# A hybrid SSD and S5 layer: residuals and half of a weight split as accumulating transfers, Silu on ScalarE

## The chip, the cores and the metric

One Trainium2 chip, one of its cores. The metric is the device time of one execution, in microseconds (us); smaller is better. The kernel is one launch, and its inputs and outputs lie in the chip's main memory.

## The reference

One layer is applied to 1024 prompt frames and to 32 frames of a running stream (1056 columns in all), 1024 channels, all in float32:

```
P = RMSNorm_pre_mix(x) @ W_in                 # -> [z | xBC | dt | u]
SSD:  xBC = silu(causal_dwconv4(xBC));  h_t = exp(dt_t a) h_{t-1} + dt_t x_t B_t^T;  y_t = C_t h_t + D x_t
      ssd = grouped RMSNorm(y * silu(z))      # 8 heads x 64, 2 groups of B and C, state 128
S5:   h_t = lb * h_{t-1} + B u_t (complex, 32 groups x 64 states);  y = Re(C h) + D u;  s5 = GLU(gelu(y))
h = x + RMSNorm_post_mix([ssd | s5] @ W_out)
[g | v] = causal_dwconv3(RMSNorm_pre_ffn(h) @ W_up)        # 2 x 2816 channels
y = h + RMSNorm_post_ffn((gelu(g) * v) @ W_down)
```

The states and the last convolution columns are returned too.

## The kernel before, in words

**Layout and tiling.** Channels lie on the 128 partitions, frames along the free axis. The frames are cut into three chunks of 512, 272 and 272 columns; the first is block 0, the other two are block 1 (544 columns). A vector of 1024 channels is eight slabs of 128 partitions. Each float32 product is made of three passes of a rounded type: an operand is split into a high half (the rounded value) and a low half (the rest), and TensorE adds high x high, high x low and low x high. Weights come as tiles of 128x1024 from the tensor wt. For each tile SP, the queue of SyncE, loads the raw values (`w_load`), ScalarE copies them into the high half `wh`, which rounds, and VectorE subtracts to get the low half `wl` (`w_split`, line 713). Each of the three names has two buffers. The tiles in order are 16 of the input projection, then the output projection and the up projection; the down projection has functions of its own.

**Stages.** `prologue` loads x, makes the two halves `xh` and `xl` (line 1045), squares each slab on ScalarE and collects the squares (`flush`): where the slab's number is in the parameter `pairs`, GpSimd adds it to the square before it, else it becomes one more tensor of a list. `norm_cols` multiplies each tensor of that list by a column of ones (`onec`), 128 frames at a time, accumulating over the list in one bank. `norm_r` turns the sums into factors by some small VectorE steps (`rsq`, lines 603 to 626) and spreads these over the partitions with one more product (`spread`). The input projection follows, with the S5 preparation and scan beside it as side work (`s5_prep`, `s5_run`). z is gated in `evac_z` and the later columns of xBC are convolved in `conv_b`, both with a sigmoid made of Tanh. `ssd_front` makes the masks of the SSD decay, exponentials on ScalarE follow. `post(b)` computes h: each slab of the output projection `O[b]` is multiplied by the norm's factor (line 1659), GpSimd adds x (line 1660), and h is split and squared for the next norm. For block 0, h is also kept in a tensor h_dram in main memory. Then two FFN blocks run; `up_evac` writes the tile fext, whose two leading columns are copied from `halo`. `fin_mm` makes the down projection's last part with the squares, and `fin_out` and `apply` the outputs: ScalarE multiplies by the norm's weight, VectorE or GpSimd (by the parameter `fp`) multiplies by the factor, then adds h (lines 1891 and 1893), and SP stores the result in yT.

**Order.** `Plan` reads all instructions and their dependences, estimates a cost for each, schedules them by lists and fixes the order in every engine's own queue. ScalarE's order is chosen with a price for each change of function table. SP alone issues the transfers, in the planned order. An instruction that waits holds back all behind it on its engine.

Of the kernel before, what the change touches and what calls it, by code (L numbers as in the profile page):

```python
# [9 lines left out]
F32 = mybir.dt.float32  # L10
# [9 lines left out]
WA = 512  # L20
# [28 lines left out]
           cvat='run7', tcat=1, late_at=2, nsq=1, fg=(), fp=((1, 3), (1, 3), (3,)), fch=(0, (0, 1), 2), pfin=0, q0=0, q1=0, q2=0, nb=0,   # L49
           hv=(), av=(3,), post0=0.802, dn_at=((3, 0), (3, 1)), ob_at=22, sa=2, sb=1, y5b=0, cvb=2.11, msb=(1, 1, 2, 2, 2), pch0=(3,),   # L50
           pch1=(3,), pch2=(3, 4), pf=0, pb=500, pg=0, pn=500, pr=0, pairs=(1, 2, 3, 5, 6), cf=4, cb=1, cg=0, cf2=2, cb2=(0, 1), cg2=0, 
# [130 lines left out]
class Plan:  # L182
# [61 lines left out]
    def read(self):  # L244
# [97 lines left out]
    def cost(self, q, i, ia, oa):  # L342
        self.eng[q] = e = str(i.engine).split(".")[-1]
        kind = type(i).__name__
        n = max(self.free(a) for a, _ in ia + oa)
        if kind == "InstDMACopy":
            self.bytes[q] = 4 * int(np.prod([m for _, m in ia[0][0].ap]))
            self.dur[q], self.lat[q] = 0.06, 2.0
            return
        if kind == "InstMatmult":  # L350
            n, m = (self.free(a) for a, _ in ia[:2])
            if ia[0][0].dtype == F32R:
                d = max(0.43 * n + 6, 107 if m > 64 else 54)
            elif i.is_transpose:
                d = 112
            else:
                d = 2 * max(0.85 * n, 108) if m > 64 else 0.85 * n
            self.dur[q], self.lat[q] = d * 1e-3, 0.07
            return
        big = [a for a, _ in ia if self.free(a) > 1]  # L360
        ps = any(g[0].startswith(("ms", "pm")) for _, g in ia)
        if kind == "InstActivation":
            self.fset[q] = str(i.func).split(".")[-1]
            d = 0.19 + 0.00085 * n + 0.08 * (len(ia) > len(big))
        elif e == "Pool":
            self.shared[q] = len(big) > 1
            d = 0.21 + 0.00165 * n if len(big) > 1 else 0.12 + 0.0009 * n
        else:
            self.shared[q] = not ps and n > 8
            d = 0.15 + (0.00105 if ps or len(big) > 1 else 0.00053) * n  # L370
        self.dur[q] = d

    def schedule(self, rank, pre, suc, forward=True, gate=None):
# [12 lines left out]
        while todo:  # L386
# [28 lines left out]
            if self.bytes[q]:  # L415
                if forward:
# [3 lines left out]
                end[q] = max(s + self.lat[q], wire + 0.8)  # L420
                lanes = lanes[1:] + [end[q]]
# [37 lines left out]
def body(tc, xT, wt, wdt, vec, cst, dtp, hist4, hist3, h0ssd, s5p, s5bc, s5d, glu, glub,  # L459
# [245 lines left out]
    def w_split(n):  # L705
        while st["split"] <= min(n, len(seq) - 1):
# [6 lines left out]
            V.tensor_tensor(lo, r, hi.bitcast(F32), sub)  # L713
# [35 lines left out]
    h_dram = dram.tile([128, KD, WA], F32, name="hd")  # L749
# [40 lines left out]
    def conv_b():  # L790
        yield par["cvat"]
        n = EB - 3
        cwh = con.tile([128, 40], F32, name="cwh")
        V.tensor_scalar(cwh, vc("cw", 0, 40), 0.5, None, mult)
        for j in range(8):
            e = XB[1][:, j, :]
            o, th = tl(("bc", "PQ")[j % 2], [128, n], "xob"), e[:, 0:n]
# [9 lines left out]
    def evac_z(j, c, ps):  # L807
# [533 lines left out]
    def ssd_front(c):  # L1341
# [301 lines left out]
    def post(b):  # L1643
        HN[b] = xtiles(b)
        for c in BLKC[b]:
# [7 lines left out]
            for j in range(4):  # L1653
                xr = iot("xr")[:, :, :w]
                D.dma_start(xr, xT[:, 2 * j:2 * j + 2, t0:t0 + w])
                for kk in range(2):
                    k = 2 * j + kk
                    h = O[b][:, k, o:o + w]
                    V.scalar_tensor_tensor(h, h, vc("post_mix", k), r1, mult, mult)  # L1659
                    (V if k in par["hv"] else G).tensor_tensor(h, h, xr[:, kk], add)  # L1660
# [9 lines left out]
                if b == 0:  # L1670
                    D.dma_start(h_dram[:, 2 * j:2 * j + 2], O[b][:, 2 * j:2 * j + 2, o:o + w])
# [188 lines left out]
    def fin_out(c):  # L1860
# [13 lines left out]
        if c == 1:  # L1874
            ap = [(1, j) for j in par["fp"][1]] + [(1, j) for j in range(4) if j not in par["fp"][1]][:par["ia"]]
        elif c == 2:
            ap = [(1, j) for j in range(4) if j not in par["fp"][1]][par["ia"]:] + ap
        with ExitStack() as es:
            if c == 2:
                es.enter_context(tc.issue_after(last[0].ins))  # L1880
            for c_, j in ap:
                apply(c_, j)
                yield 0.9

    def apply(c, j):
# [13 lines left out]
    hrs = {}  # L1899

    def fin_block(b):
        if b == 0:
            for j, n in enumerate(("ext0", "ext1", "W0", "G0", "T0", "C0")):
                h = tl(n, [128, 2 if j < 2 else 1, 512], "hr")
                k = 2 * j if j < 2 else j + 2
                D.dma_start(h, h_dram[:, k:k + h.shape[1]])
                for i in range(h.shape[1]):
                    hrs[k + i] = h[:, i]
# [37 lines left out]
```

## Time and profile before

| | |
|---|---|
| median of the runs | 1296.92 us (1296.79 to 1300.04) |
| the profiled execution | 1294.34 us, its span 1292.4 us |
| mean granted clock of TensorE | 0.979 |
| TensorE busy (matmul) | 1225.8 us, 95% |
| VectorE busy | 1035.2 us, 80% |
| ScalarE busy | 574.5 us, 44% |
| GpSimd busy | 397.7 us, 31% |
| main memory read, written | 111.69 MB, 15.81 MB |

The busy times are those of one profiled execution; the span runs from its first to its last instruction, and the execution's own time has 1.9 us more around it. PE is TensorE, DVE VectorE, ACT ScalarE, POOL GpSimd, and SP the engine that issues the transfers. The granted clock is the share of full speed at which TensorE was allowed to run.

### The profile page before, as it was taken

What the parts mean: (1) busy time and instruction counts of PE and PEld (TensorE: products, weight loads), DVE (VectorE), ACT (ScalarE), POOL (GpSimd) and SP (SyncE); (2) the same over time, 40 slices, a digit from 0 to 9 for tenths busy, and PEclk for the clock granted to TensorE, in tenths of its full rate; (3) what the DMA queues carried; (4) which work ended last, traced back from release to release, by engine and by line L of the source; (5) the groups of instructions that cost most, each with busy time, mean ns of one, the idle gap of its engine ahead of it and who ended that gap; (6) DMA issues with size and microseconds to landing.
All of it is one profiled execution on the core that took longest, in us unless ns stands there. A gap on an engine that the chain in (4) does not pass through costs nothing.

```text
span 1292.4 us, 20981 instructions
## 1 busy us (share of the span) xinstructions
PE 1225.8 (95%) x7880; PEld 1105.6 (86%) x7880; DVE 1035.2 (80%) x1781; ACT 574.5 (44%) x979; POOL 397.7 (31%) x577
## 2 busy tenths in 40 slices
PE   6879999999998999999999999998999999999995
PEld 5768888888877888878977888887999999999994
DVE  7898887988988998987688977679577777777777
ACT  7236466554555555543444433353523333333243
POOL 5364554544146433211345110015111111111113
PEclk8989999999998999999999999999999999999997
DMA  7133323233434423234433333222323332222212
GB/s 220 57 96 99 96 76 114 79 106 93 124 105 164 152 91 99 81 104 137 153 99 123 122 99 98 95 85 82 117 81 98 99 98 82 95 86 83 82 52 70
DMA packets 66901, 132.14 MB, mean 102 GB/s; under 512 B 13936, under 2 KB 34800, under 8 KB 66800
## 3 DMA queue, kind: packets, MB, share of 16 engines
q1 hardware_dynamic: 66800, 130.81, 32.2%
q8 instruction: 62, 1.02, 0.3%
q14 instruction: 39, 0.32, 0.1%
HBM read 111.69 MB, written 15.81 MB: 99 GB/s over the span
## 4 chain that ended last, share of the span: by engine, by line
PE 79%; DVE 10%; POOL 3%; issue 3%; DMA 2%; ACT 1%; SPq 1%; DVEq 0%; ACTq 0%; POOLq 0%
PE pm L479 70%; PE ms L479 9%; DVE wl L713 1%; POOL pacc L1666 1%; POOL o L1660 1%; DVE o L1659 1%; SPq L1122 1%; DMA xst<-xT 1%; DVE scr L647 1%; DVE scr L646 1%; POOL oacc L1628 1%; PE ms L483 1%; DVE pq L996 1%; POOL hq L1164 0%; DVE yr L1104 0%
## 5 line engine op out<-in xcount | busy, mean ns | idle before, releaser
L479 PE MATMUL pm<-xh,wh 128*128 128x272 f32 (+1 forms) x1616 | 532.1, 330 | 15.9 <-ACT wh L535 8.7
L479 PE MATMUL pm<-xh,wl 128*128 128x272 f32 (+1 forms) x1616 | 531.1, 329 | 7.4 <-DVE wl L713 7.3
L479 PE MATMUL pm<-xl,wh 128*128 128x272 f32 (+1 forms) x1616 | 529.8, 328 | 1.7 <-DVE xl L1045 1.7
L479 PEld LDWEIGHTS pm<-xh,wh 128*128 128x128 f32 x1616 | 309.9, 192 | 37.8 <-ACT wh L535 8.7
L479 PEld LDWEIGHTS pm<-xh,wl 128*128 128x128 f32 x1616 | 309.0, 191 | 30.8 <-DVE wl L713 9.1
L479 PEld LDWEIGHTS pm<-xl,wh 128*128 128x128 f32 x1616 | 309.9, 192 | 24.4 <-DVE xl L1045 3.0
L535 ACT ACTIVATE wh<-raw 128x1024 fp32r<-128x1024 f32 x120 | 126.9, 1057 | 177.5 <-PE pm L479 109.5
L713 DVE TENSOR_TENSOR wl<-raw,wh 128x1024 fp32r<-128x1024 f32 x120 | 154.9, 1291 | 26.6 <-ACT wh L535 26.1
L479 PE MATMUL pm<-al,dh 128*128 128x272 f32 (+1 forms) x528 | 171.4, 325 | 0.6 <-DVE al L1751 0.6
L479 PE MATMUL pm<-ah,dh 128*128 128x272 f32 (+1 forms) x528 | 171.7, 325 | 0.3 <-ACT ah L535 0.3
L479 PE MATMUL pm<-ah,dl 128*128 128x272 f32 (+1 forms) x528 | 170.8, 324 | 0.0
L1793 DVE TENSOR_TENSOR acc<-acc,pm 128x272 f32<-128x272 f32 (+1 forms) x235 | 121.1, 520 | 53.6 <-PE pm L479 52.5
L1738 DVE SCALAR_TENSOR_TENSOR ftmp<-fext,vec_t,ftmp 128x512 f32<-128x512 f32 (+1 forms) x176 | 143.1, 814 | 3.9 <-ACT ftmp L535 2.1
L1716 POOL COPY fext<-halo 128x2 f32<-128x2 f32 x88 | 33.6, 382 | 293.0 <-DVE ftmp L1738 271.5
L1721 DVE TENSOR_TENSOR fext<-pm,rbc 128x512 f32<-128x512 f32 (+2 forms) x132 | 67.5, 511 | 69.2 <-PE pm L479 65.8
L479 PEld LDWEIGHTS pm<-ah,dh 128*128 128x128 f32 x528 | 99.4, 188 | 8.6 <-ACT ah L535 0.7
L479 PEld LDWEIGHTS pm<-al,dh 128*128 128x128 f32 x528 | 99.3, 188 | 8.1 <-DVE al L1751 0.9
L479 PEld LDWEIGHTS pm<-ah,dl 128*128 128x128 f32 x528 | 99.2, 188 | 7.7 <-issue 0.3
L535 ACT ACTIVATE dh<-raw 128x1024 fp32r<-128x1024 f32 (+1 forms) x46 | 46.7, 1018 | 108.3 <-PE pm L479 96.8
L535 ACT ACTIVATE ftmp<-fext,vec_t 128x512 f32<-128x512 f32 (+1 forms) x88 | 72.3, 822 | 11.1 <-DVE fext L1721 5.7
L535 ACT ACTIVATE ftmp<-ftmp 128x512 f32<-128x512 f32 (+1 forms) x44 | 28.4, 644 | 87.0 <-DVE ftmp L1738 87.0
L1771 DVE TENSOR_TENSOR dl<-raw,dh 128x1024 fp32r<-128x1024 f32 (+1 forms) x46 | 55.9, 1216 | 13.6 <-ACT dh L535 13.6
(318 smaller groups left out, 1668.7 us busy)
## 6 DMA issues: line engine op xcount, KB each, us to landing
raw<-wt SPq DMA_DIRECT2D x164, 512.0 KB, 3.3
gluw<-glu SPq DMA_DIRECT2D x8, 512.0 KB, 3.4
xst<-xT SPq DMA_DIRECT2D x16, 136.0 KB, 3.3
pbd<-pbo SPq DMA_DIRECT2D x8, 272.0 KB, 2.6
xr<-xT SPq DMA_DIRECT2D x8, 272.0 KB, 3.2
pbi<-pbd SPq DMA_DIRECT2D x8, 272.0 KB, 3.5
yT<-acc SPq DMA_DIRECT2D x8, 272.0 KB, 2.3
ud<-uext SPq DMA_DIRECT2D x4, 528.0 KB, 4.0
```

Source lines behind the costliest of these rows:

```text
L479: PE.matmul(out, lhsT, rhs, start=start, stop=stop, **kw)
L483: PE.transpose(out, in_, ident)
L535: S.activation(out, in_, func, bias=bias, scale=scale)
L646: e.tensor_scalar(hi[:L, o:o + L], ident[:L, :L], r[:L, i:i + 1], None, mult)
L647: last[0] = V.scalar_tensor_tensor(lo[:L, o:o + L], ident[:L, :L], r[:L, i:i + 1], hi[:L, o:o + L].bitcast(F32), mult, sub)
L713: V.tensor_tensor(lo, r, hi.bitcast(F32), sub)
L996: V.tensor_scalar(pq[lo:hi, a], src[lo:hi, :, o:o + 8], sg, None, mult)
L1716: G.tensor_copy(e[:, 0:2], halo[:, j, :])
L1721: V.tensor_tensor(e[:, 2 + o:2 + o + wp], ps[:, :wp], rbc[:, t0:t0 + wp], mult)
L1738: V.scalar_tensor_tensor(t, e[:, i:i + n], vc("fw", 3 * j + i), t, mult, add)
L1771: V.tensor_tensor(l, rr, h.bitcast(F32), sub)
L1793: V.tensor_tensor(a, a, ps[:, :w], add)
```

## The change

It has seven parts.

1. *First squares.* `pairs` is empty: the eight squares of the first block go to `norm_cols` as eight tensors instead of three, without GpSimd's additions.
2. *Weight tiles.* For the tiles 3 to 15 of the order, ScalarE writes minus the rounded value into `lo`, and a transfer issued by GpSimd reads the same tile of wt again and adds it to `lo` on landing.
3. *Gate of z and later convolution.* Silu replaces Tanh with the operations around it.
4. *Decay masks.* Each of the two tensors of a chunk is made by eight GpSimd operations of 128x128 with one scalar for each partition, instead of one operation on two tensors.
5. *h.* The slab pair is multiplied in place, then a transfer issued by GpSimd adds x to it. h is stored in yT for both blocks by SP; h_dram and the loads of x into `xr` go.
6. *Outputs.* The factor is read from PSUM without ScalarE's copy; every multiplication is VectorE's (`fp` is empty); a transfer issued by GpSimd adds the result to yT, where h already lies. The loads of h, the additions and the moving of some multiplications from one chunk to the next go.
7. *Plan.* Reads of PSUM by one engine keep their order, transfers of GpSimd have their own costs (1.0 us, 3.5 us), and matmul costs change a little.

```diff
-           cvat='run7', ..., fp=((1, 3), (1, 3), (3,)), ...
+           cvat='run7', ..., fp=((), (), ()), ...
-           pch1=(3,), ..., pairs=(1, 2, 3, 5, 6), ...
+           pch1=(3,), ..., pairs=(), ...
...
+                if g[0].startswith(("ms", "pm")):
+                    self.pre[q].update(k for k, h in r.get(g[0], ()) if self.eng[k] == self.eng[q])
...
-            self.dur[q], self.lat[q] = 0.06, 2.0
+            self.dur[q], self.lat[q] = (0.06, 2.0) if e == "SP" else (1.0, 3.5)
...
-                d = max(0.43 * n + 6, 107 if m > 64 else 54)
+                d = max(0.426 * n + 9, 107 if m > 64 else 54)
...
             act(hi, r, AF.Copy)
-            V.tensor_tensor(lo, r, hi.bitcast(F32), sub)
+            if 3 <= i < 16:
+                act(lo, r, AF.Copy, scale=-1.0)
+                G.dma_start(lo, wt[seq[i]], accum_op=add)
+            else:
+                V.tensor_tensor(lo, r, hi.bitcast(F32), sub)
...
     def conv_b():
...
-            act(o, e[:, 0:n], AF.Identity, scale=cwh[:, 4 * j:4 * j + 1], bias=cwh[:, 32 + j:33 + j])
+            act(o, e[:, 0:n], AF.Identity, scale=vc("cw", 4 * j), bias=vc("cb", j))
             for i in range(1, 4):
-                V.scalar_tensor_tensor(o, e[:, i:i + n], cwh[:, 4 * j + i:4 * j + i + 1], o, mult, add)
-            act(th, o, AF.Tanh)
-            V.scalar_tensor_tensor(e[:, 0:n], th, 1.0, o, add, mult)
+                V.scalar_tensor_tensor(o, e[:, i:i + n], vc("cw", 4 * j + i), o, mult, add)
+            act(e[:, 0:n], o, AF.Silu)
...
-        V.scalar_tensor_tensor(zt, ps, 0.5, rbc[:, t0:t0 + w], mult, mult)
-        act(ps, zt, AF.Tanh)
-        V.scalar_tensor_tensor(zt, ps, 1.0, zt, add, mult)
+        V.tensor_tensor(zt, ps, rbc[:, t0:t0 + w], mult)
+        act(zt, zt, AF.Silu)
...
-        ub = upper[:L, None, :L].to_broadcast([L, 8, L])
         for dst, src in ((rh, DT["ah"]), (rl, DT["al"])):
-            G.tensor_tensor(dst, src[:L, c].bitcast(F32)[:, :, None].to_broadcast([L, 8, L]), ub, mult)
+            for h in range(8):
+                G.tensor_scalar(dst[:, h, :], upper[:L, :L], src[:L, c, h:h + 1].bitcast(F32), None, mult)
...
-                D.dma_start(xr, xT[:, 2 * j:2 * j + 2, t0:t0 + w])
+                for kk in range(2):
+                    h = O[b][:, 2 * j + kk, o:o + w]
+                    V.scalar_tensor_tensor(h, h, vc("post_mix", 2 * j + kk), r1, mult, mult)
+                G.dma_start(O[b][:, 2 * j:2 * j + 2, o:o + w], xT[:, 2 * j:2 * j + 2, t0:t0 + w], accum_op=add)
                 for kk in range(2):
...
-                    V.scalar_tensor_tensor(h, h, vc("post_mix", k), r1, mult, mult)
-                    (V if k in par["hv"] else G).tensor_tensor(h, h, xr[:, kk], add)
...
-                if b == 0:
-                    D.dma_start(h_dram[:, 2 * j:2 * j + 2], O[b][:, 2 * j:2 * j + 2, o:o + w])
+                D.dma_start(yT[:, 2 * j:2 * j + 2, t0:t0 + w], O[b][:, 2 * j:2 * j + 2, o:o + w])
...
-        r = fin[c][0]
...
-            act(r, norm_r(fin[c], w, scrt(...), G if c in par["fg"] else None, f"f{c}"), AF.Copy)
+            fin[c] = [norm_r(fin[c], w, scrt(...), None, f"f{c}")]
...
-        e = G if j in par["fp"][c] else V
-        e.tensor_tensor(a, a, fin[c][0][:, None, :].to_broadcast([128, 2, w]), mult)
-        if b:
-            e.tensor_tensor(a, a, O[b][:, 2 * j:2 * j + 2, o:o + w], add)
-        else:
-            for kk in range(2):
-                e.tensor_tensor(a[:, kk], a[:, kk], hrs[2 * j + kk], add)
-        D.dma_start(yT[:, 2 * j:2 * j + 2, t0:t0 + w], a)
+        V.tensor_tensor(a, a, fin[c][0][:, None, :].to_broadcast([128, 2, w]), mult)
+        G.dma_start(yT[:, 2 * j:2 * j + 2, t0:t0 + w], a, accum_op=add)
```

## Rows read from the trace of the kernel before

**Rows 1.** The page's chain that ended last, shares of the span by engine.
```profile
PE 79%; DVE 10%; POOL 3%; issue 3%; DMA 2%; ACT 1%; SPq 1%; DVEq 0%; ACTq 0%; POOLq 0%
```

**Rows 2.** Stretches: length, PE, PEld, DVE, ACT, POOL busy (count), clock, DMA share, GB/s.
```profile
0.00:66.00 66.00, 51.16 (x271) 44.16 (x272) 52.95 (x136) 33.16 (x66) 29.46 (x65) 0.92 0.44 137
66.00:102.00 36.00, 27.19 (x158) 22.44 (x157) 33.44 (x46) 13.51 (x29) 22.48 (x22) 0.86 0.38 113
102.00:260.00 158.00, 149.80 (x1039) 138.64 (x1038) 133.17 (x229) 88.87 (x204) 78.34 (x85) 0.99 0.31 88
260.00:396.00 136.00, 130.62 (x836) 113.08 (x835) 113.58 (x178) 70.09 (x128) 52.39 (x40) 0.99 0.38 111
396.00:432.00 36.00, 31.50 (x216) 30.18 (x216) 33.64 (x37) 20.76 (x39) 28.70 (x16) 0.93 0.52 181
650.00:705.00 55.00, 51.43 (x245) 40.47 (x245) 47.74 (x96) 26.69 (x51) 33.10 (x37) 1.00 0.38 115
880.00:903.00 23.00, 17.55 (x132) 16.77 (x131) 21.30 (x34) 6.85 (x8) 15.10 (x13) 0.92 0.29 104
903.00:1263.00 360.00, 360.00 (x2861) 360.00 (x2861) 261.06 (x477) 128.98 (x192) 49.70 (x162) 1.00 0.27 87
1263.00:1292.40 29.40, 13.51 (x104) 12.35 (x103) 21.25 (x47) 8.45 (x20) 11.24 (x8) 0.70 0.22 76
```

**Rows 3.** The tile wl on VectorE: 60 to 305 us, then 102 to 260.
```profile
L713 DVE TENSOR_TENSOR wl<-raw,wh x13: 1212/1221/1710, 61.8 to 301.4; 128x1024 fp32r<-128x1024 f32 x13
...
L713 DVE TENSOR_TENSOR wl<-raw,wh x9: 1212/1218/1660, 107.7 to 258.2; 128x1024 fp32r<-128x1024 f32 x9
```

**Rows 4.** The tile wh on ScalarE, 140 to 305 us.
```profile
L535 ACT ACTIVATE wh<-raw x9: 1043/1060/1070, 146.5 to 300.4; 128x1024 fp32r<-128x1024 f32 x9
```

**Rows 5.** Line 814: durations (ns, min/median/max), first and last start.
```profile
L814 DVE SCALAR_TENSOR_TENSOR zst<-pm,zst x12: 415/440/684, 267.3 to 345.1; 128x272 f32<-128x272 f32 x8, 128x512 f32<-128x512 f32 x4
```

**Rows 6.** Groups by line and shape, whole span: count, busy us, mean ns.
```profile
L1349 POOL TENSOR_TENSOR rh<-dtah,cst_t 128x1024 fp32r<-128x1024 f32 x8 | 16.6, 2074 | 18.0 <-DVE R L1162 11.1 <-PE ms L479 6.9
...
L1045 DVE SCALAR_TENSOR_TENSOR xl<-xst,vec_t,xh 128x512 fp32r<-128x512 f32 x8 | 9.7, 1259 | 3.1 <-ACT xh L535 3.1
...
L802 DVE SCALAR_TENSOR_TENSOR xb<-xb,xob 128x547 f32<-128x547 f32 x8 | 6.6, 826 | 0.0
```

**Rows 7.** ScalarE's timeline, 262 to 445 us: start, duration.
```profile
276.27 1.28 ACT L535 ACT_TABLE_LOAD   x1
...
441.59 1.28 ACT L535 ACT_TABLE_LOAD   x1
```

**Rows 8.** Waits, 400 to 420 us: who waited for whom, us, times, longest.
```profile
PE pm L479 <- DVE wl L713: 4.2, 1, 4.2
```

**Rows 9.** VectorE's timeline, 386 to 436 us.
```profile
401.77 9.92 DVE L1659 SCALAR_TENSOR_TENSOR o<-o,vec_t,oacc 128x512 f32<-128x512 f32 x7 [1.22 <-ACT oacc L535]
```

**Rows 10.** GpSimd's timeline, 386 to 436 us.
```profile
402.60 6.85 POOL L1660 TENSOR_TENSOR o<-o,xr 128x512 f32<-128x512 f32 x4 [5.40 <-DVE o L1659]
```

**Rows 11.** Waits, 880 to 903 us.
```profile
PE pm L479 <- DVE fext L1721: 4.1, 1, 4.1
```

**Rows 12.** VectorE's timeline, 1276 to 1293 us.
```profile
1277.07 1.05 DVE L606 TENSOR_SCALAR nry<-nrt 128x3 int32<-128x3 int32 x1
1278.15 0.16 DVE L620 TENSOR_TENSOR nra<-nry 128x3 f32<-128x3 f32 x1
...
1282.89 0.72 DVE L1891 TENSOR_TENSOR acc<-acc,sacc 128x544 f32<-128x544 f32 x1 [0.40 <-ACT sacc L535]
...
1285.31 1.85 DVE L1891 TENSOR_TENSOR acc<-acc,sacc 128x544 f32<-128x544 f32 x1
```

**Rows 13.** The timeline of all engines, 0 to 62 us: products of the first squares.
```profile
20.80 3.64 PE L479 MATMUL ms<-onec,xst 128*128 128x1 f32 x22
```

**Rows 14.** Transfers: size, median us from issue to landing.
```profile
raw<-wt SPq DMA_DIRECT2D x164, 512.0 KB, 3.3
...
yT<-acc SPq DMA_DIRECT2D x8, 272.0 KB, 2.3
```

More of the change, by code (lines that the diff above doesn't have):

```diff
@@ L48 @@
            run3=0.5, uload=6.619, swap_pool=1, z_s5=1, ssd0=13.784, ssd1=0.0, ssd2=2.778, gate0=76.032, glu0=0.384, glu1=2.807, abufs=2,
-           cvat='run7', tcat=1, late_at=2, nsq=1, fg=(), fp=((1, 3), (1, 3), (3,)), fch=(0, (0, 1), 2), pfin=0, q0=0, q1=0, q2=0, nb=0,
+           cvat='run7', tcat=1, late_at=2, nsq=1, fg=(), fp=((), (), ()), fch=(0, (0, 1), 2), pfin=0, q0=0, q1=0, q2=0, nb=0,
            hv=(), av=(3,), post0=0.802, dn_at=((3, 0), (3, 1)), ob_at=22, sa=2, sb=1, y5b=0, cvb=2.11, msb=(1, 1, 2, 2, 2), pch0=(3,),
-           pch1=(3,), pch2=(3, 4), pf=0, pb=500, pg=0, pn=500, pr=0, pairs=(1, 2, 3, 5, 6), cf=4, cb=1, cg=0, cf2=2, cb2=(0, 1), cg2=0,
+           pch1=(3,), pch2=(3, 4), pf=0, pb=500, pg=0, pn=500, pr=0, pairs=(), cf=4, cb=1, cg=0, cf2=2, cb2=(0, 1), cg2=0,
            pgt=500, p5at=1, ng=0, n12=(2, 0), cho=2, dtlag=112.5, ng2=1, pairs2=(1, 2, 3, 5, 6, 7))
@@ L415, in schedule @@
             if self.bytes[q]:
-                if forward:
+                if forward and e == "SP":
                     s = max(s, lanes[0])
@@ L419, in schedule @@
                 wire = max(wire, s + 0.9) + self.bytes[q] / 280e3
-                end[q] = max(s + self.lat[q], wire + 0.8)
-                lanes = lanes[1:] + [end[q]]
+                end[q] = max(s + self.dur[q] + self.lat[q], wire + 0.8)
+                if e == "SP":
+                    lanes = lanes[1:] + [end[q]]
             else:
@@ L748, in body @@
     pb_dram = dram.tile([128, KD, T - WA], F32, name="pbd")
-    h_dram = dram.tile([128, KD, WA], F32, name="hd")
     ext4 = {}
@@ L792, in conv_b @@
         n = EB - 3
-        cwh = con.tile([128, 40], F32, name="cwh")
-        V.tensor_scalar(cwh, vc("cw", 0, 40), 0.5, None, mult)
         for j in range(8):
             e = XB[1][:, j, :]
-            o, th = tl(("bc", "PQ")[j % 2], [128, n], "xob"), e[:, 0:n]
-            act(o, e[:, 0:n], AF.Identity, scale=cwh[:, 4 * j:4 * j + 1], bias=cwh[:, 32 + j:33 + j])
+            o = tl(("bc", "PQ")[j % 2], [128, n], "xob")
+            act(o, e[:, 0:n], AF.Identity, scale=vc("cw", 4 * j), bias=vc("cb", j))
             for i in range(1, 4):
-                V.scalar_tensor_tensor(o, e[:, i:i + n], cwh[:, 4 * j + i:4 * j + i + 1], o, mult, add)
-            act(th, o, AF.Tanh)
-            V.scalar_tensor_tensor(e[:, 0:n], th, 1.0, o, add, mult)
+                V.scalar_tensor_tensor(o, e[:, i:i + n], vc("cw", 4 * j + i), o, mult, add)
+            act(e[:, 0:n], o, AF.Silu)
             yield par["cvb"]
@@ L1864, in fin_out @@
         yield 3
-        r = fin[c][0]
         with tc.high_priority(par["pn"]):
-            act(r, norm_r(fin[c], w, scrt(*(("xo", "Z0"), ("xo", "W1"), ("T1", "G1"))[c]), G if c in par["fg"] else None, f"f{c}"),
-                AF.Copy)
+            fin[c] = [norm_r(fin[c], w, scrt(*(("xo", "Z0"), ("xo", "W1"), ("T1", "G1"))[c]), None, f"f{c}")]
         yield 1
@@ L1873, in fin_out @@
         ap = [(c, j) for j in range(4)]
[L1874 to L1883, printed above, removed]
+        for c_, j in ap:
+            apply(c_, j)
+            yield 0.9
     def apply(c, j):
@@ L1889, in apply @@
         a = ACC[b][:, 2 * j:2 * j + 2, o:o + w]
-        e = G if j in par["fp"][c] else V
-        e.tensor_tensor(a, a, fin[c][0][:, None, :].to_broadcast([128, 2, w]), mult)
-        if b:
-            e.tensor_tensor(a, a, O[b][:, 2 * j:2 * j + 2, o:o + w], add)
-        else:
-            for kk in range(2):
-                e.tensor_tensor(a[:, kk], a[:, kk], hrs[2 * j + kk], add)
-        D.dma_start(yT[:, 2 * j:2 * j + 2, t0:t0 + w], a)
-    hrs = {}
-    def fin_block(b):
[L1902 to L1908, printed above, removed]
+        V.tensor_tensor(a, a, fin[c][0][:, None, :].to_broadcast([128, 2, w]), mult)
+        G.dma_start(yT[:, 2 * j:2 * j + 2, t0:t0 + w], a, accum_op=add)
+    def fin_block(b):
         for c in BLKC[b]:
```

## Prediction

> **What bounds the kernel now.** I read the chain of waits first. It runs through TensorE for 79% of the span and through VectorE for 10% [rows 1], so work taken off another engine counts only where TensorE stands still for that engine. The table by stretches shows where that is [rows 2]: TensorE is idle for 66.0 - 51.2 = 14.8 us up to 66, 8.8 us to 102, 8.2 us to 260, 5.4 us to 396, 4.5 us to 432, 3.6 us from 650 to 705, 5.5 us from 880 to 903, and 15.9 us after 1263. From 903 to 1263 it is busy for 360 of 360 us, and nothing in that stretch can be gained. In most stretches with idle time VectorE is busy 80 to 93%. The granted clock falls with the idle time: 0.86 in 66 to 102, 0.93 in 396 to 432, 0.92 in 880 to 903, against 1.00 where TensorE does not stop; that is a mixture of the full level of 2.4 GHz and the half one of 1.2 GHz, so a wait there costs more than itself.
>
> One thing more is to be seen. The same VectorE multiplication of 128x544 takes 0.72 us by itself and 1.85 us in the midst of GpSimd's additions [rows 12]. GpSimd's additions are therefore paid for by VectorE too.
>
> **Part by part.**
>
> *First squares (up to 66 us).* The block's eight squares went to the sum as three tensors; now as eight. There are four groups of columns and two records for each product, so 64 records instead of 24: 40 more at 3.64/22 = 0.165 us [rows 13], 6.6 us of TensorE, nearly all of it behind the last square because the groups of one bank follow one another. Against it, five GpSimd additions go, and with them the slowing of the eight low halves of x: 1.26 us each [rows 6] against some 0.70 for 512 columns (scaled from 0.72 for 544), 4.5 us of VectorE. I take +2 us, between -4.5 and +6.6.
>
> *Thirteen low halves (61.8 to 302.6 us).* VectorE loses one operation of 1.22 us for each [rows 3], ScalarE gets a second copy of 1.06 us [rows 4], and GpSimd issues a 512 KB transfer that adds into the tile. Its queue waits there for ScalarE's copy; behind it stand the outer products of the S5 preparation and the product hq. Nothing in the trace is an accumulating transfer. Its landing is bounded below by the plain one of 512 KB, 3.3 us [rows 14], and above by three such legs one after another (read, read, write), 9.9 us. I take 1.0 us of issue on GpSimd and 3.5 us to land, the figures that the diff gives its own planner, near the plain row. A low half is then ready some 1.06 + 4.5 - 1.22 = 4.3 us later than now. What hides it is the second buffer: the tiles follow at (301.4 - 61.8)/12 = 20 us [rows 3]. Without that cover each of the 13 would cost 4.3 us.
>
> Nine of the operations lie in 102 to 260 [rows 3], 11.0 us out of 133.2 of VectorE's work. TensorE's 8.2 us there are waits on the S5 chain, which passes through VectorE several times for each group. I take half of them, -4 us, between 0 and -8.2. In 66 to 102 one operation goes: -1 us, between 0 and -8.8.
>
> *Silu and the decay masks (260 to 396 us).* VectorE loses 12 x 0.44 = 5.3 us of the gate [rows 5], 8 x 0.826 = 6.6 us of the later convolution [rows 6], and two low halves, 2.4 us. Two GpSimd operations of 2.07 us a chunk [rows 6] become sixteen on 128x128; at an eighth each that is the same GpSimd time, plus sixteen starts instead of two, and no row shows whether VectorE suffers less beside them: 0. ScalarE now runs Silu between the exponentials of the decay; today it loads no function table between 276.3 and 441.6 us [rows 7], and a load takes 1.28 us. For five chunks, two loads each, that is 12.8 us, on an engine that is busy for 70 of 136 us there. TensorE idles for only 5.4 us. I take 0, between -5.4 and +12.8.
>
> The Trainium skill (ScalarE: Activation LUTs, What ACT_TABLE_LOAD costs) counts about 2.66 us for each change of set, because a drain comes on top of the load, and asks for calls grouped by set. The trace agrees on the load, 1.28 us; it does not show the drain as a row. By that page ten changes would be an estimated 26.6 us of ScalarE instead of 12.8.
>
> *Residual before the FFN, first block (396 to 432 us).* Seven multiplications of 128x512 take 9.92 us beside GpSimd's residual additions, four of which take 6.85 us [rows 9, 10]; then a weight tile's low half is late and TensorE waits 4.2 us for it [rows 8]. Without the additions the eight multiplications need 8 x 0.70 = 5.6 us, until 407.4 instead of past 411.7, so the low half (1.22 us) is there some 4 us sooner and the wait goes. The clock of 0.93 costs 2.5 us of the 36, most of which goes too: -6 us. What is late next is the sum h itself: each of four slabs lands 4.5 us after its multiplication, where GpSimd took 2 x 1.71 us and then still had to add squares. That evens out. Bounds: -7 and, at three legs, +7 (see the first rival).
>
> *The same, second block (650 to 705 us).* GpSimd loses sixteen smaller additions and TensorE's idle time is 3.6 us; but the norms' products stand in TensorE's fixed order and wait for the last slab. Behind the issuing instruction on GpSimd stand the additions of squares and the small halo copies; SP's eight new stores of h wait for the landing with weight loads behind them, but SP's loads of x go. I take 0, between -3.6 and +10.
>
> *Outputs (880 to 903 us).* Two of four slab multiplications and the additions of two slabs move off GpSimd, and the additions off VectorE: four multiplications of 128x1024 stay, about 1.35 us each (scaled from 0.72 for 544), with no two-tensor work beside them. TensorE's one long wait is 4.1 us for VectorE [rows 11], and the clock of 0.92 costs 1.8 us: -5 us, between 0 and -6.
>
> *The end.* The last chunk's factor is ready at 1282.89; one of the small steps before it took 1.05 us beside GpSimd instead of the usual 0.16, and the copy of 0.40 us goes [rows 12]. So about 1281.6, four multiplications of 0.75 us, 1284.6, then issue and landing of 4.5 us: 1289.1 instead of 1292.4. I take -3 us, between -5 and +8 (two plain legs of 2.3 us for each of four slabs in series, [rows 14], from 1281.6 + 0.75 + 1.0 on: 1301.8, less what overlaps).
>
> Elsewhere 0: the planner's changed costs reorder all queues, which no row prices.
>
> Sum: +2 - 1 - 4 + 0 - 6 + 0 - 5 - 3 = -17 us. The profiled execution took 1294.34 us for a span of 1292.4; the sum gives 1277.3 for it. The median of the runs is 1296.92, 2.6 us above, so I forecast 1280 us.
>
> **The rivals.**
>
> *The transfers land late.* Speaking for it: each reads its target too. At two legs a 512 KB landing is 6.6 us; if four slabs go in series that is 26.4 us against eight additions of 1.71 us = 13.7 us, 12.7 us more, and the first block's stretch is +7 instead of -6; the second about +10 instead of 0; the end +8 instead of -3. With the other terms: +2 - 1 - 4 + 0 + 7 + 10 - 5 + 8 = +17, or 1314 us. Against it: the transfer engines are busy only 22 to 52% in these stretches [rows 2]. From -17 at 3.5 us to +17 at 6.6 us, it decides from a landing of about 5 us on: slower than before.
>
> *Table loads on the path.* If all ten loads delay the decay's exponentials and TensorE behind them, the 260 to 396 stretch is +12.8, and the time 1293. For it: Silu and Exp alternate. Against: ScalarE has 66 us free there.
>
> With the page's drain, the estimate would be 1307 us; I give that no more than a part of this rival's chance.
>
> *VectorE's relief is hidden.* Only waits that name VectorE or GpSimd go: +2 - 6 - 5 - 3 = -12, 1285 us. For it: TensorE carries 79% of the chain. Against: VectorE is above 80% in every stretch with waits.
>
> *The relief comes back whole.* All idle time of 66 to 396 and of 650 to 705 goes: +2 - 8.8 - 8.2 - 5.4 - 6 - 3.6 - 5 - 3 = -38, 1259 us. Against: the waits pass through ScalarE and GpSimd as well.
>
> *New order, new stalls.* Four waits like the 4.2 us one eat the gain: 1297 us.
>
> **How the numbers follow.** Forecast 0.48; late landing 0.12; table loads 0.08; hidden relief 0.17; whole relief 0.10; new stalls 0.05. About 0.3% (3.9 us) is what a measurement can tell. Faster are the forecast, the hidden and the whole relief and part of the table loads: 0.80; same 0.07; slower 0.13. The range of 1262 to 1297 leaves out the late landing and about half of the whole relief. The likeliest case alone is 1270 to 1287.
>
> **What would show it.** TensorE's 4.2 us wait for a low half in 400 to 420 gone, and that of 4.1 us for fext; VectorE's residual multiplications at about 0.7 us instead of 1.4; its busy time down by 40 us or more. New rows of transfers issued by GpSimd: 1 us of issue and under 5 us to land confirm the sum, above 5 us the first rival. Between 276 and 441 some ten table loads. If TensorE waits for a weight's accumulated low half, the two buffers did not cover it, and the forecast is wrong; so it is if the products of the first squares delay everything behind them by more than 6.6 us.

## The result

The change made the kernel slower: 1385.82 us (median of four runs, 1379.6 to 1394.38) against 1298.48 us before (four runs), a ratio of 1.0675 with a 95% interval of 1.0613 to 1.0737. The forecast was 1280 us. The profiled execution is the slowest of the four, 1394.38 us with a span of 1392.6; it lies 8.6 us above the median, so the stretches read from it below add up to 100.2 us more than before, where the medians differ by 87.3.

The page of the changed kernel, busy time by engine and the chain by engine (before: 95, 86, 80, 44 and 31% busy; the chain is that of [rows 1]):

```profile
PE 1262.5 (91%) x7920; PEld 1139.4 (82%) x7920; DVE 961.4 (69%) x1743; ACT 612.4 (44%) x1011; POOL 419.1 (30%) x699
...
PE 71%; issue 8%; DVE 7%; POOL 5%; DMA 4%; ACT 3%; SPq 1%; POOLq 0%; ACTq 0%; DVEq 0%
```

VectorE lost 74 us of work, and yet the time grew. The part of the chain that is new is "issue", 8% instead of 3%: time in which an engine stood still and the profile shows nothing that it waited for.

To see where the time went I set marks where TensorE had done 15, 25, 30, 47.5, 55, 65, 70 and 100% of its columns, in the kernel before and in the changed one. These are the stretches between the marks, without 30 to 47.5 and 55 to 65%, where the two differ by 1.9 and 0.0 us. The columns are those of [rows 2]; first the kernel before:

```profile
0.00:247.30 247.30, 215.45 (x1372) 193.17 (x1373) 207.19 (x391) 130.23 (x288) 123.34 (x163) 0.95 0.36 106
247.30:379.00 131.70, 127.85 (x848) 111.81 (x847) 116.08 (x184) 70.10 (x131) 48.05 (x42) 1.00 0.36 105
379.00:449.30 70.30, 64.27 (x389) 57.75 (x389) 59.91 (x76) 34.30 (x57) 44.01 (x27) 0.95 0.44 148
659.30:753.10 93.80, 90.42 (x411) 72.52 (x410) 83.09 (x151) 39.95 (x65) 34.80 (x44) 1.00 0.36 111
866.50:933.20 66.70, 61.26 (x442) 58.98 (x442) 50.28 (x78) 31.96 (x55) 25.43 (x32) 0.95 0.28 95
933.20:1281.80 348.60, 342.68 (x2733) 342.15 (x2732) 258.52 (x489) 122.90 (x182) 49.97 (x152) 0.99 0.26 84
1281.80:1292.40 10.60, 0.63 (x2) 0.00 (x0) 7.01 (x7) 0.40 (x1) 3.56 (x2) 0.50 0.38 131
```

and the changed kernel:

```profile
0.00:260.90 260.90, 224.39 (x1407) 202.50 (x1408) 198.88 (x381) 146.75 (x302) 113.64 (x169) 0.95 0.46 119
260.90:415.50 154.60, 141.03 (x845) 121.36 (x844) 94.15 (x157) 87.11 (x146) 82.18 (x108) 0.91 0.36 95
415.50:507.90 92.40, 70.63 (x382) 63.70 (x381) 43.74 (x78) 37.03 (x60) 42.72 (x45) 0.82 0.46 125
719.80:831.90 112.10, 95.37 (x411) 77.55 (x410) 77.00 (x152) 41.25 (x69) 25.80 (x38) 0.89 0.43 109
945.30:1011.20 65.90, 63.65 (x441) 61.50 (x440) 43.06 (x75) 31.68 (x54) 14.57 (x30) 0.92 0.42 97
1011.20:1357.30 346.10, 342.69 (x2736) 342.07 (x2736) 255.58 (x491) 122.52 (x181) 43.46 (x150) 0.99 0.26 83
1357.30:1392.60 35.30, 0.68 (x2) 0.00 (x0) 2.62 (x4) 0.00 (x0) 8.26 (x7) 0.50 0.48 55
```

The loss has five places: +13.6 us up to the first mark, +22.9 in the gates and the SSD fronts, +22.1 and +18.3 in the two stretches of the residual before the FFN, and +24.7 after TensorE's last column. The granted clock falls where TensorE waits, from 0.95 to 0.82 in the third stretch: of its 22.1 us TensorE is busy for 6.4 us longer with as many columns.

The third and the fourth place have one cause. In the waits of TensorE, 415 to 508 us and 719 to 832 us:

```profile
PE ms L482 <- POOL pacc L1669: 8.9, 1, 8.9
PE ms L482 <- DVE btsc L1370: 8.3, 1, 8.3
...
PE ms L482 <- POOL pacc L1669: 16.7, 2, 9.0
```

The norm's product waits for GpSimd's sum of squares of h (`pacc`), and GpSimd's own timeline, 438 to 482 us, shows why that is late:

```profile
443.59 1.25 POOL L1660 DMA_DIRECT2D o<-xT  x1 [14.39 <-DVE o L1659]
450.20 1.22 POOL L1660 DMA_DIRECT2D o<-xT  x1 [5.36 <-issue]
458.86 1.21 POOL L1660 DMA_DIRECT2D o<-xT  x1 [7.44 <-issue]
466.84 1.20 POOL L1660 DMA_DIRECT2D o<-xT  x1 [6.76 <-PE pm L482]
```

The waits of GpSimd over the whole span put a sum to it:

```profile
POOL o L1660 <- issue: 27.2, 6, 7.4
```

An issue is busy for 1.2 us, but the next one begins 6.6 to 8.7 us later, although VectorE had finished all eight multiplications at 447.1. VectorE's timeline, then ScalarE's, 438 to 482 us:

```profile
441.72 5.39 DVE L1659 SCALAR_TENSOR_TENSOR o<-o,vec_t,oacc 128x512 f32<-128x512 f32 x8 [2.01 <-ACT oacc L538]
...
458.61 0.63 ACT L538 ACTIVATE xr<-o 128x512 f32<-128x512 f32 x1 [6.94 <-DMA o<-xT]
```

The second row belongs to the other long wait of the third place, 8.3 us for `btsc`, a tile of the SSD part. ScalarE stood 6.94 us for a slab of h to land; behind that in its queue stood the copy of a weight tile, VectorE's low half waited for the copy, and `btsc` came behind the low half. So this wait hangs on the same transfers.

The same distance between issues stands at the end, in GpSimd's timeline 1352 to 1393 us, with half the bytes:

```profile
1357.04 1.21 POOL L1884 DMA_DIRECT2D yT<-acc  x1 [3.70 <-DVE scr L642]
...
1362.10 1.22 POOL L1884 DMA_DIRECT2D yT<-acc  x1 [3.84 <-issue]
...
1386.63 1.21 POOL L1884 DMA_DIRECT2D yT<-acc  x1 [3.63 <-issue]
```

Eight issues follow at 4.9 us, and their data take 4.6 us to land (the transfers' table, size and median time from the start of the issue to the landing):

```profile
wl<-wt POOLq DMA_DIRECT2D x13, 512.0 KB, 6.4
o<-xT POOLq DMA_DIRECT2D x8, 272.0 KB, 4.6
yT<-acc POOLq DMA_DIRECT2D x8, 272.0 KB, 4.6
o<-xT POOLq DMA_DIRECT2D x4, 512.0 KB, 8.0
```

So each issue comes about when the transfer before it has landed. For the second place other rows stand out, groups by line and form over the whole span (count, busy us, mean ns) of the function tables and the masks; 12 of the 40 table loads lie between 260.9 and 415.5 us, where the kernel before has one in the same stretch:

```profile
L538 ACT ACT_TABLE_LOAD x40 | 51.3, 1283 | 8.9 <-DMA xst<-xT 4.3 <-DVE yr L902 4.0
...
L1351 POOL TENSOR_SCALAR rh<-cst_t,dtah 128x128 fp32r<-128x128 f32 x64 | 51.0, 812 | 20.9 <-DVE R L1164 20.2 <-DVE o L1624 0.7
L1351 POOL TENSOR_SCALAR rl<-cst_t,dtal 128x128 fp32r<-128x128 f32 x64 | 48.5, 772 | 41.2 <-PE ms L482 23.7 <-DVE xl L1540 14.7 <-ACT TC L538 2.7
```

An eighth of a mask takes 0.79 us in the mean, where the whole took 2.07 [rows 6].

### The profile page after: what moved, and what is told of

Its sections match the earlier page's. It is cut to its first block, busy times and chain, and to the rows that moved or that the text cites. A ratio compares the mean times of both kernels' runs of the same rounds, so it can differ in the third digit from the quotient of the medians.

```text
span 1392.6 us, 21176 instructions
## 1 busy us (share of the span) xinstructions
PE 1262.5 (91%) x7920; PEld 1139.4 (82%) x7920; DVE 961.4 (69%) x1743; ACT 612.4 (44%) x1011; POOL 419.1 (30%) x699
## 4 chain that ended last, share of the span: by engine, by line
PE 71%; issue 8%; DVE 7%; POOL 5%; DMA 4%; ACT 3%; SPq 1%; POOLq 0%; ACTq 0%; DVEq 0%
PE pm L482 62%; PE ms L482 8%; POOL rh L1351 2%; DMA o<-xT 1%; DMA Traw<-kd 1%; DVE yr L1106 1%; SPq L1124 1%; POOL rl L1351 1%; DVE o L1659 1%; DMA ug<-ud 1%; ACT L538 1%; POOL yT L1884 1%; DMA zd<-zst 0%; SPq L1530 0%; POOL pacc L1669 0%
## 5 line engine op out<-in xcount | busy, mean ns | idle before, releaser
L482 PEld LDWEIGHTS pm<-xh,wh 128*128 128x128 f32 x1616 | 313.0, 194 | 26.7 <-DVE uext L764 2.7
L482 PEld LDWEIGHTS pm<-xl,wh 128*128 128x128 f32 x1616 | 313.2, 194 | 22.8 <-issue 1.2
L720 DVE TENSOR_TENSOR wl<-raw,wh 128x1024 fp32r<-128x1024 f32 x107 | 132.0, 1233 | 41.0 <-ACT wh L538 40.7
L1740 DVE SCALAR_TENSOR_TENSOR ftmp<-fext,vec_t,ftmp 128x512 f32<-128x512 f32 (+1 forms) x176 | 137.5, 781 | 23.8 <-ACT ftmp L538 21.4
L538 ACT ACTIVATE ftmp<-fext,vec_t 128x512 f32<-128x512 f32 (+1 forms) x88 | 72.2, 821 | 33.7 <-DVE fext L1723 13.5
L1735 POOL COPY o<-fext 128x2 f32<-128x2 f32 x44 | 9.9, 230 | 187.5 <-DVE fext L1723 187.5
```

The source lines that it names most:

```text
L482: PE.matmul(out, lhsT, rhs, start=start, stop=stop, **kw)
L538: S.activation(out, in_, func, bias=bias, scale=scale)
L1740: V.scalar_tensor_tensor(t, e[:, i:i + n], vc("fw", 3 * j + i), t, mult, add)
```

## The experiments

**One part undone at a time.** All start from the changed kernel.

```diff
 a_noacc: post and fin_out/apply/fin_block as before, with fp=((1, 3), (1, 3), (3,)) and h_dram
 a_nomask (ub as in the kernel before):
-            for h in range(8):
-                G.tensor_scalar(dst[:, h, :], upper[:L, :L], src[:L, c, h:h + 1].bitcast(F32), None, mult)
+            G.tensor_tensor(dst, src[:L, c].bitcast(F32)[:, :, None].to_broadcast([L, 8, L]), ub, mult)
 a_nolo:
-            if 3 <= i < 16:
...
+            V.tensor_tensor(lo, r, hi.bitcast(F32), sub)
 a_nosilu: conv_b and evac_z as before
```

> The changed kernel with the residuals and the outputs as before (additions by GpSimd and VectorE, stores by SP, two or one of four slab multiplications by GpSimd); the rest of the change stays. Theory 1 (accumulating transfers of GpSimd run one at a time, each issue waiting for the landing before it): TensorE's lag that grows by 24 us around 450 to 508, by 18 us around 733 to 783 and the 25 us more after TensorE's last product go, some 67 us: 1305 to 1335 us. Theory 2 (the loss lies in the new order of the queues, or in the masks and low halves): above 1355 us.

> The changed kernel with the decay masks in one operation on two tensors each, as before. Theory 3 (sixteen small GpSimd operations for each chunk cost some 104 us of GpSimd instead of 34, and TensorE's lag of 24 us between 283 and 350 comes from that): 1355 to 1372 us, and the lag in that stretch gone. Rival (GpSimd has room there, the lag is that of ScalarE's table loads or of the queue order): 1378 to 1395 us.

> The changed kernel with all low halves by VectorE, as before. Theory 4 (the accumulated low halves, which land 6.4 us after their issue and stand in the queues of ScalarE and GpSimd, make TensorE's lag of 21 us between 102 and 283): 1358 to 1370 us. Rival (the lag there is the S5 chain's in another order; the two buffers cover the low halves): 1378 to 1395 us.

> The changed kernel with Tanh and the operations around it instead of Silu, in the gate of z and in the later convolution, as before. If the 22 added table loads of 1.28 us (28 us of ScalarE) stand on TensorE's path: 1358 to 1378 us. If ScalarE's free time hides them: 1380 to 1400 us, since VectorE gets 12 us of work back.

Measured: 1331.32, 1359.87, 1369.08 and 1383.25 us, that is 54.5, 26.0, 16.7 and 2.6 us less than the changed kernel. The loss that theories 1 and 3 speak of is where they place it: without the accumulating transfers of h and of the outputs the two residual stretches and the end lose 2.5, 0.0 and 0.1 us instead of 22, 18 and 25; with whole masks the second place loses 1.2 instead of 23, and the third 15 instead of 22. Whether the issues really wait for landings, as theory 1 says, these runs do not show yet. Theory 4 has its number, but see below. The table loads of Silu, with VectorE's relief against them, cost nothing to be seen: 1383.25 lies within the changed kernel's runs. These runs and those below come from several chips, on which the kernel before had medians of 1297.5 to 1301.8 us, and the changed kernel's own runs spread over 14.8 us; a difference of a few us between two of them says little.

**The planner and the parts by themselves.** Now from the kernel before.

```diff
 b_plan, b_lo, b_sq (the change's planner lines for transfers besides):
+                if g[0].startswith(("ms", "pm")):
+                    self.pre[q].update(k for k, h in r.get(g[0], ()) if self.eng[k] == self.eng[q])
...
-                d = max(0.43 * n + 6, 107 if m > 64 else 54)
+                d = max(0.426 * n + 9, 107 if m > 64 else 54)
 b_lo besides: w_split of the change
 b_sq besides: conv_b and evac_z of the change, pairs=()
```

> The kernel before with the planner's new costs and rules alone, nothing else of the change. If the new order of the queues is harmless by itself: 1290 to 1305 us. If the order is a cause of its own: above 1310 us.

> The kernel before with the planner's new costs and the thirteen low halves by ScalarE and an accumulating transfer. Theory 4 (the low halves alone make the lag of 66 to 283 us): 15 to 20 us above the kernel with the new planner alone. Rival (what undoing them gave back was another order in the presence of the masks): within 5 us of it.

> The kernel before with the planner's new costs, Silu in the gate and the later convolution, and all eight first squares by TensorE; no accumulating transfer, no small mask operations. Undoing Silu gave 2.5 us back, so Silu costs next to nothing in time: -5 to +5 us against the kernel with the new planner alone; by the prediction's terms +2 for the squares and 0 for Silu.

Measured: b_plan 1306.77 us (ratio 1.0067, 1.0037 to 1.0097), b_lo 1309.12, b_sq 1301.21. The planner's edits alone cost some 9 us, in the gap between my two expectations; the low halves alone add 2.4, so theory 4 falls here. b_sq is 5.6 us below b_plan, just outside what I expected.

**Room for descriptors.** GpSimd writes the descriptors of its transfers into a reserved piece of SBUF, of 1024 bytes per partition in both kernels. The Trainium skill (DMA: Bandwidth & Descriptors, SWDGE vs HWDGE vs iDMA) says that the rings of these descriptors lie in SBUF.

```diff
-    nc = bacc.Bacc("TRN2", ..., dynamic_dma_scratch_size=1024)
+    nc = bacc.Bacc("TRN2", ..., dynamic_dma_scratch_size=2048)
-    hist3_t = con.tile([128, 2 * FF, 2], F32, name="hist3_t")
-    D.dma_start(hist3_t, hist3)
+    D.dma_start(o3[:, :, 1, :], hist3)
```

> The changed kernel with 2048 instead of 1024 bytes for each partition of memory in which GpSimd writes the descriptors of its transfers (room made by keeping the old convolution columns hist3 in the tile of the new ones). Theory 5 (the memory holds one transfer's descriptors, and the next issue waits until they are read): at the end the eight issues follow at some 2.5 instead of 4.9 us, TensorE's waits in both residual stretches shrink, and the time is 1340 to 1365 us. Rival (accumulating transfers wait for each other whatever the room): the pitch stays at 4.9 us, 1378 to 1395 us.

Measured: 1327.72 us, 58.1 less than the changed kernel, by this edit alone, and more than theory 5 expected. GpSimd's timeline at the end of that kernel:

```profile
1307.41 3.78 POOL L1883 DMA_DIRECT2D yT<-acc  x3 [2.38 <-DVE acc L1794]
1312.25 1.20 POOL L1883 DMA_DIRECT2D yT<-acc  x1 [1.06 <-DVE scr L642]
...
1316.06 1.21 POOL L1883 DMA_DIRECT2D yT<-acc  x1 [0.18 <-issue]
1317.70 1.20 POOL L1883 DMA_DIRECT2D yT<-acc  x1 [0.42 <-issue]
1319.98 1.20 POOL L1883 DMA_DIRECT2D yT<-acc  x1 [1.08 <-issue]
```

Three issues stand together and the rest follow at 1.4 to 2.4 us. In this trace each of the rest starts some 0.3 us after the landing of the third transfer before it; in the changed kernel's each starts some 0.3 us after the landing of the one before it. The transfers by themselves, with little and with much room:

```diff
 q_1024, q_16384: only transfers and the copies between their groups; two of the four groups; a, b, u, w are tiles
+        for t0 in (512, 784):
+            for j in range(4):
+                G.dma_start(yT[:, 2 * j:2 * j + 2, t0:t0 + 272], a[...], accum_op=add)
...
+                G.dma_start(yT[:, 2 * j:2 * j + 2, t0:t0 + 272], b[...])
```

> No layer at all, only transfers, in four groups that wait for each other: eight accumulating ones of 272 KB from SBUF to yT, four accumulating ones of 512 KB into SBUF, then the same numbers plain, all issued by GpSimd, with 1024 bytes for each partition for descriptors. Theory 5 (room for descriptors): the accumulating stores follow at 4.9 us as at the end of the changed kernel, and the plain ones wait for room as well, at 3 to 5 us. Rival (accumulation makes them wait): the accumulating ones at 4.9 us, the plain ones at the issue's own 1.2 us.

> The same transfers with 16384 bytes for each partition. Theory 5: the accumulating stores follow at 1.2 to 2 us, the cost of the issue itself; the landing of each grows, as they share the transfer engines. Rival: still 4.9 us.

GpSimd's timeline with 1024 bytes, accumulating (from a), plain (from b), and accumulating into whole weight tiles w; then its transfers' table:

```profile
27.09 1.37 POOL L203 DMA_DIRECT2D yT<-a  x1 [26.64 <-DMA yT<-a]
32.08 1.26 POOL L203 DMA_DIRECT2D yT<-a  x1 [3.62 <-issue]
36.89 1.21 POOL L203 DMA_DIRECT2D yT<-a  x1 [3.55 <-issue]
...
83.56 2.21 POOL L213 DMA_DIRECT2D yT<-b  x3
86.49 0.73 POOL L213 DMA_DIRECT2D yT<-b  x1 [0.72 <-issue]
...
91.45 2.84 POOL L208 DMA_DIRECT2D w<-wt  x3 [0.31 <-issue]
97.10 0.86 POOL L208 DMA_DIRECT2D w<-wt  x1 [2.82 <-issue]
...
yT<-a POOLq DMA_DIRECT2D x8, 272.0 KB, 4.7
yT<-b POOLq DMA_DIRECT2D x8, 272.0 KB, 2.8
```

and with 16384 bytes, with the line of the eight accumulating issues (durations in ns, min/median/max, first and last start) and their landings:

```profile
26.73 10.01 POOL L203 DMA_DIRECT2D yT<-a  x8 [26.28 <-DMA yT<-a]
...
59.80 5.84 POOL L213 DMA_DIRECT2D yT<-b  x8
...
L203 POOL DMA_DIRECT2D yT<-a x8: 1371/2982/4717, 26.7 to 32.0; - x8
...
DMA to landing us min/median/max: 4.7/8.4/10.8
```

With room the eight accumulating issues stand in one piece and start 0.76 us apart, (32.0 - 26.7)/7; with 1024 bytes they start 4.8 to 5.1 us apart. Each then takes longer, up to 10.8 us to land instead of 4.7, and still the last one has landed 16.1 us after the first issue, against 39.6 with 1024 bytes. Plain ones of the same size wait for room as well, but only from the fourth on and for 0.2 to 0.7 us, not at the 3 to 5 us from issue to issue that I expected. So theory 5 holds, and its rival falls. Accumulation counts in one way: with 1024 bytes three plain transfers of 272 KB fit where one accumulating one does.

What fills the room is not the bytes moved. Of the accumulating transfers into whole weight tiles, 512 KB each, three stand together with the same 1024 bytes, whereas those of x into h in the changed kernel, 512 KB too, came one at a time. In the program the first have one row of 4 KB for each partition, the second two rows of 2 KB. That the number of rows decides fits these cases; no run varies it by itself.

**What the other parts cost once there is room.** Both have 2048 bytes.

```diff
 c_ttmask: the masks of a_nomask
 c_resid: the masks of a_nomask and the low halves of a_nolo
```

> The changed kernel with 2048 bytes for descriptors and with the decay masks in one operation each, as before. If the two effects add up: 1327.7 - 26 = 1302 us, 1294 to 1310 us. If the masks' cost was only the blocked queue of GpSimd: 1318 to 1330 us.

> The same, and with all low halves by VectorE, as before: what stays of the change are the accumulating residuals and outputs, Silu, the first squares and the planner's costs. If undoing the low halves still gives 17 us: 1278 to 1293 us, faster than the kernel before. If the low halves cost only the 2.4 us that they cost alone: 1295 to 1305 us.

Measured: 1305.97 and 1301.26 us. The masks' 21.7 us add to the room's 58; the low halves give 4.7. By the medians that is together 84.6 of the 87.3 us that the change cost.

```diff
 e_both: 1024 bytes, masks of a_nomask, low halves of a_nolo
 e_s2nolo: 2048 bytes, small masks, low halves of a_nolo
```

> The changed kernel with the decay masks in one operation each and the low halves by VectorE, both as before, and 1024 bytes for descriptors. With the masks alone undone it took 1359.9 us. If the low halves are dear because of the room: 1340 to 1347 us. If because of the mask operations on the same queue: 1352 to 1358 us.

> The changed kernel with 2048 bytes for descriptors and the low halves by VectorE, the small mask operations kept. With room alone it took 1327.7 us. If the low halves are dear because of the mask operations: 1308 to 1315 us. If because of the room: 1320 to 1326 us.

Measured: 1354.13 and 1310.03 us. With small masks the low halves cost 16.7 and 17.7 us, without them 5.7 and 4.7, whatever the room. The numbers are those that I expected of a shared queue, but the place is not: most of what comes back lies in the first stretch (next table), and the changed kernel's first mask operation starts at 260.7 us, at its very end. So I take it that the masks act there through the order that the planner makes; no run shows that by itself.

**The rest, and a faster kernel.**

```diff
 b_rule: b_plan with the old line d = max(0.43 * n + 6, ...)
 b_silu: b_sq with the old pairs
 d_fin: b_sq with the old line of b_rule, 2048 bytes, the change's outputs, and in apply
+        if c < 2:
+            G.dma_start(yT[:, 2 * j:2 * j + 2, t0:t0 + w], a, accum_op=add)
+        else:
+            (G if j == 3 else V).tensor_tensor(a, a, O[b][:, 2 * j:2 * j + 2, o:o + w], add)
+            D.dma_start(yT[:, 2 * j:2 * j + 2, t0:t0 + w], a)
 d_fin3: the same with c < 1, and GpSimd adding for (c, j) = (1, 1) and (1, 3)
```

> The kernel before with the planner's rule that reads of PSUM by one engine keep their order, and the old matmul cost. If the rule makes the 9 us of the planner's edits: 1303 to 1309 us. If the new matmul cost makes them: 1294 to 1301 us, like before.

> The kernel before with the planner's new costs and Silu in the gate and the later convolution, first squares as before. With the squares too it took 1301.2 us, and 1306.8 us with the planner's costs alone. By the prediction's terms (squares +2, Silu 0 to a small gain) 1297 to 1301 us; if the eight squares on TensorE are what helped: 1304 to 1309 us.

> The kernel before with the rule (old matmul cost), Silu, the eight first squares and 2048 bytes for descriptors; the outputs of the first two chunks by accumulating transfers, those of the last chunk with additions and stores by SP; masks, low halves and the residuals before the FFN as before. The two kernels with accumulating outputs and room gained 7 to 8 us where the first block's outputs lie. From 1301 us with Silu and squares: 1290 to 1297 us, faster than before. If that gain is given back at the end: 1297 to 1303 us.

> The same with accumulating outputs for the first chunk alone, the other two with additions and stores by SP. If the gain is that of the first block's outputs: as the one before, within 3 us; if the second chunk's transfers delay the end: 2 to 5 us faster than that.

Measured: b_rule 1301.68 us, b_silu 1304.6, d_fin 1285.85 (ratio 0.9906, 0.9888 to 0.9925), d_fin3 1286.33. b_rule lies between my two expectations: of the planner's 9 us the rule on PSUM, with the lines for transfers, keeps about 4 (ratio 1.0031, 1.0015 to 1.0047), and the matmul cost would be the other 5, but the interval overlaps that of b_plan. Silu and squares: 1306.8, 1304.6, 1301.2, steps of about the size of the spread. d_fin is 0.9% faster than the kernel before. It keeps the accumulating outputs of the first two chunks, Silu, the first squares, the rule and the room, and leaves out the small masks, the low halves, the accumulating residuals, the new matmul cost and the accumulating transfers at the end. In its profile 6.5 of the 9.2 us lie where the first block's outputs are, and d_fin3, with those of the first chunk alone, is as fast, as expected if the gain is theirs. The same kernel without these outputs was not run.

The change of each stretch against the kernel before, us, from one profiled execution each (the changed kernel's is its slowest, so its row is high):

| kernel | to 15% | 15 to 25% | 25 to 30% | 47.5 to 55% | 65 to 70% | after 100% | span |
|---|---|---|---|---|---|---|---|
| changed | +13.5 | +23.0 | +22.1 | +18.3 | -0.8 | +24.6 | +100.2 |
| a_noacc | +13.1 | +20.6 | +2.5 | 0.0 | +0.8 | +0.1 | +38.4 |
| a_nomask | +12.4 | +1.2 | +15.0 | +18.2 | -4.4 | +24.4 | +65.9 |
| a_nolo | -2.1 | +14.9 | +22.7 | +18.1 | -2.8 | +24.3 | +74.8 |
| a_nosilu | +15.6 | +12.5 | +21.9 | +18.4 | -2.8 | +23.6 | +91.3 |
| a_s2048 | +11.7 | +16.6 | +6.4 | +3.2 | -6.5 | +2.9 | +33.9 |
| e_s2nolo | -5.3 | +14.6 | +7.8 | +2.0 | -7.9 | +3.2 | +14.1 |
| e_both | +8.8 | -0.7 | +15.7 | +18.1 | -2.5 | +24.3 | +61.9 |
| c_ttmask | +11.9 | +4.0 | +1.3 | +1.2 | -7.9 | +3.2 | +11.6 |
| c_resid | +7.1 | -0.7 | +2.5 | +4.9 | -6.5 | +2.8 | +8.8 |
| b_plan | +14.2 | +0.4 | -0.4 | -1.5 | +0.8 | 0.0 | +13.9 |
| b_lo | +7.4 | +8.0 | +0.1 | -0.1 | -0.1 | +0.1 | +15.0 |
| d_fin | +2.7 | -1.3 | -2.1 | +1.6 | -6.5 | -0.1 | -9.2 |

## Why the prediction was wrong

**The step that failed first** is the overlap of the accumulating transfers. The prediction took "I take 1.0 us of issue on GpSimd and 3.5 us to land", so 4.5 us in all, for each transfer as if it stood alone, and let the next slab's issue follow at once. The price of one was near for 272 KB: 1.2 us of issue, landed 4.6 us after the issue began. For 512 KB it was too low, 5.5 to 8.4 us. What I put at nothing without a reason is the wait for room between two issues. They came at 4.9 to 8.7 us, since the descriptors of the next one had no room. The changed planner makes the same assumption: it counts only SP's transfers against its limit of transfers under way, and GpSimd's against none. The three terms that rest on it, -6, 0 and -3, came out as +22, +18 and +25; with twice the room they are +6, +3 and +3, so some 53 of these 65 us are the room, and the medians give 58. The plain row that I chose [rows 14] was transferred by SP and told nothing of GpSimd's queue. The Trainium skill (DMA: Bandwidth & Descriptors, Anatomy of one DMA) gives 2.0 us and bytes over 436e3 for a transfer issued by GpSimd, an estimated 2.6 us for 272 KB. The plain transfers alone show 2.8 us, which agrees; the accumulating ones show 4.7 us in the same run.

**My first rival** had the right mechanism in outline, late landing and slabs in series, and the right sign. It made the series out of slower legs on the transfer engines and its three terms of +7, +10 and +8 were 25 us; the series was in the issues, which its argument against it, transfer engines busy only 22 to 52%, does not touch, and the three came to 65.

**The masks.** That "at an eighth each that is the same GpSimd time" is the second step that failed. The prediction named the "sixteen starts instead of two" and gave them no price. The whole operation took 2.07 us for 1024 elements a partition [rows 6], the eighth takes 0.79 us in the mean instead of 0.26: 99.5 us for 128 of them, instead of some 33 for sixteen whole ones. The stretch from 15 to 25% grew by 12 to 23 us in every kernel that has them, and by 8 at most in those without.

**The planner at 0** was the third: its edits alone cost 9 us, in its profile nearly all up to the first mark. There the kernels lie between -5 and +16 us, by the order that the planner found as far as I can see; it also holds what undoing the low halves gives back. Which row of that order costs the time stays open.

**What held.** The two named waits of TensorE, 4.2 us for a low half and 4.1 us for fext, are gone. The two buffers covered the low halves all but once: TensorE waited 1.4 us for one, between 260 and 416 us. VectorE's relief came: 74 us in all, residual multiplications of 0.75 us and low halves of x of 0.75 where I said 0.70. It was worth nothing where GpSimd's queue took its place as what is late next. The outputs' -5 is -6.5 to -7.9 once there is room, -0.8 to -4.4 with 1024 bytes. The end's gain before the last transfers is there (-2.5 between 70 and 100%) and is lost to them. Silu's 0 and the squares' +2 lie within the spread; 12 table loads fall between 276 and 441 us, near the ten, and 22 more than before in the whole span, at no cost that the runs can tell. Two readings of rows were off, though no term that failed rests on them: the 0.72 us row at 1282.89 [rows 12] is not VectorE by itself, since GpSimd multiplies from 1282.94 to 1284.81, and in the last stretch VectorE is busy 72%, not above 80 [rows 2].

The rows for these, low halves and multiplications by form:

```profile
L1047 DVE SCALAR_TENSOR_TENSOR xl<-xst,vec_t,xh 128x512 fp32r<-128x512 f32 x8 | 5.8, 750 | 6.9 <-ACT xh L538 6.8
...
L1659 DVE SCALAR_TENSOR_TENSOR o<-o,vec_t,oacc 128x512 f32<-128x512 f32 x8 | 5.4, 746 | 2.0 <-ACT oacc L538 2.0
```

and TensorE's wait for a low half, from its waits between 260 and 416 us:

```profile
PE pm L482 <- DMA wl<-wt: 1.4, 1, 1.4
```

## What to carry to other kernels

A transfer that moves to GpSimd brings a queue with a capacity of its own: before its landing is priced, ask how many of them can be under way at once, and read the distance between issues, not their busy time. An operation cut into eight need not cost an eighth each; look for rows of small operations on the same engine before pricing it. And where a planner fixes every queue, an edit of its costs is a change by itself, to be run alone before anything is laid at the door of the parts.

## What the runs showed of the hardware

With 1024 bytes per partition of descriptor room GpSimd had one accumulating transfer of 272 KB under way at a time (two rows for each partition), or three plain ones of the same shape, or three accumulating ones of 512 KB with one row for each partition. With 2048 bytes it had three accumulating ones of two rows. Until there is room GpSimd stands still, with no wait in the profile but "issue": in the runs of transfers alone 5.0 us from issue to issue for 272 KB, in the mean, against 0.76 us with 16384 bytes. An accumulating store of 272 KB landed 4.7 us after its issue began, a plain one after 2.8, in the same run; with eight accumulating ones under way at once the last took 10.8 us. A GpSimd operation on 128x128 with one scalar per partition took 0.79 us in the mean, more than a third of one on 128x1024 with two tensors (2.07).
